# A Mamba-2 and latent attention trunk: the input read in a second, transposed layout, its norms spread by TensorE

## The chip, the cores and the metric

The kernel runs on one core of a Trainium2 chip. The metric is the device time of one execution in microseconds (us), as the median of several runs. A core has TensorE (PE, matrix products, with PEld for its weight loads), VectorE (DVE), ScalarE (ACT), GpSimd (POOL) and SyncE (SP, which here issues most DMAs). Each works through its own queue in order; semaphores tie them together.

## What is computed

A sequence of 2048 tokens of width 1024 passes a Mamba-2 layer and a multi-head latent attention layer, each with an RMS norm ahead and a residual add behind, and a last norm. Only the entry of the Mamba layer matters here:

```python
def rms_norm(x, g):
    y = xf * lax.rsqrt(jnp.mean(xf * xf, axis=-1, keepdims=True) + EPS)
    return (y * g.astype(jnp.float32)).astype(x.dtype)
...
hn = rms_norm(h, g_pre[l])
proj = h @ w_in
z, xBC, dt_raw = jnp.split(proj, [D_INNER, D_INNER + CONV_DIM], axis=-1)
xBC = jax.nn.silu(causal_depthwise_conv(xBC, conv_w, conv_b))
dt = jax.nn.softplus((dt_raw + dt_bias).astype(jnp.float32))
```

The norm of a token is one number, r, by which its whole row is multiplied; g_pre is one number per input channel. Behind the projection come a causal convolution over four tokens, a chunked scan with 32 heads in four groups, a gate SiLU(z), a norm per group and the output projection. Products of float32 accuracy are made of three passes: each factor is split into a high and a low part, and high times high, high times low and low times high are summed (`mm3`, lines 83 to 87).

## The kernel before, in words

The Mamba layer (`mamba`, line 224) takes the tokens in four blocks of 512 (b = 0 to 3), and each block's heads in four groups (g = 0 to 3). The input of a block has to lie with its channels on the partitions, as eight slices k of 128 channels by 512 tokens: `xT`, eight buffers for the high and the low halves.

`load_x` (line 296) loads four row tiles of 128 tokens by 1024 channels (tag `hx`, four buffers), squares them on ScalarE with a sum (line 163), works out r with thirteen small VectorE operations (`rsqrt`, line 139), and multiplies the rows by r on VectorE (line 310). `prep` (line 312) then transposes them: for each slice four TensorE transposes into one PSUM bank (line 171), and from there a split into `xT` by ScalarE (line 111) and VectorE (line 112), which also multiplies by g_pre.

`xbc` (line 324) multiplies the slices with the weight columns of B and C (two channel tiles) and then of x (four channel tiles), each bank of 128 channels by 512 tokens; the weights come through `wraw` (three raw buffers) and are split into `wsp` (six buffers). A finished bank is copied to `craw` (three buffers, line 352), gets the last three tokens of the block before it from `halo` (lines 351 and 353, GpSimd), passes four taps (lines 356 and 358) and SiLU (lines 360 and 361). `zgate` (line 367) does the gate with tokens on the partitions (lines 381 and 382). `steps` (line 416) makes the step sizes of all heads: 16 products with a weight tile `wdt` that is loaded and split once (lines 190, 201, 202, 423), a long chain of small operations, and three products with a triangle and ones (lines 463 to 465). `ssd` (line 479) is the scan, in four chunks of 128 tokens, and begins each chunk with a transpose of B (line 515). `outp` (line 388) multiplies by the output weights and adds into the residual rows `hs`, which are loaded anew from x in the first group of each block (line 394).

The order of the work comes from two places. `mamba` interleaves generators: during the scan of group g of block b it traces the output projection of the group before and the projections of the group after, and in the last but one group of a block also `load_x` (at its start), `prep` and `steps` (at its end) of the next block. The tile framework then plans at build time: it takes that order as the priority, starts what its own estimates of time call ready, and gives the buffers of a tag out in the traced order. On the chip each engine's order is fixed.

## Time and profile before

| | |
|---|---|
| median of 3 runs | 3239.51 us (3238.54 to 3240.34) |
| the profiled execution | 3238.15 us, its span 3236.3 us |
| TensorE busy | 3156.2 us (98%) |
| VectorE busy | 2593.4 us (80%) |
| ScalarE busy | 2055.2 us (64%) |
| GpSimd busy | 646.2 us (20%) |
| granted TensorE clock | 0.995 of full speed |

The span is what the profile sees between the first and the last instruction. A busy time is a union of instruction times, and matmuls overlap, so a busy TensorE need not be at its peak. In the lists of waits, a row says who waited for whom, for how long in total, how often, and the longest. Rows that group instructions give the line, the engine, the operation, the tiles written and read, the count, then the busy time and the mean duration in ns, then the idle time of the engine just before them and who ended it. A line can be that of a helper: every transpose of rows is line 171, every split lines 108 to 112.

### The profile page before, as it was taken

Reading aid. Unit: us, or ns where it says so; the run is one execution under the profiler, and the core shown is the slowest. Engines: PE = TensorE matmul, PEld = TensorE weight load, DVE = VectorE, ACT = ScalarE, POOL = GpSimd, SP = SyncE. Lnnn points to the kernel's source line nnn. Section 1 sums busy time; section 2 is a strip of 40 time slices with the busy share of each in tenths; the row PEclk is TensorE's granted clock in tenths of the full one; section 3 lists DMA queues with packets and bytes.
Section 4 is the critical chain, followed back from the end, with each engine's and each line's share of the span. In section 5 each row is a group of like instructions: output and inputs, shape, how many; then the busy total and the mean of one; then the engine's idle time right before and its main releaser. Section 6 shows DMA issues by size and latency. Waiting matters only on the chain.

```text
span 3236.3 us, 50476 instructions
## 1 busy us (share of the span) xinstructions
PE 3156.2 (98%) x16708; PEld 2563.4 (79%) x16708; DVE 2593.4 (80%) x5490; ACT 2055.2 (64%) x5117; POOL 646.2 (20%) x842
## 2 busy tenths in 40 slices
PE   8999999999999999998999999999999999999998
PEld 6788888888888888887888888777777777777787
DVE  6988888889889888887776765668888888888675
ACT  5666666666657655666555554567777877778522
POOL 1221122221212222222211211222212212223100
PEclk9999999999999999999999999999999999999999
DMA  5333343333433334333466666753443434344385
GB/s 174 108 104 92 118 131 119 105 96 122 140 96 109 90 125 145 104 94 111 132 221 212 236 204 208 246 137 79 82 89 77 97 77 88 77 90 116 81 272 172
DMA packets 210572, 418.91 MB, mean 129 GB/s; under 512 B 27107, under 2 KB 68835, under 8 KB 208869
## 3 DMA queue, kind: packets, MB, share of 16 engines
q1 hardware_dynamic: 168900, 291.39, 28.9%
q0 software_dynamic: 41408, 124.29, 15.7%
q8 instruction: 132, 2.16, 0.3%
q14 instruction: 132, 1.07, 0.1%
HBM read 321.33 MB, written 94.24 MB: 128 GB/s over the span
## 4 chain that ended last, share of the span: by engine, by line
PE 44%; ACT 3%; DMA 2%; DVE 2%; issue 1%; SPq 0%; POOL 0%; ACTq 0%; DVEq 0%
PE mm L85 7%; PE mm L87 7%; PE mm L86 7%; PE tr L933 6%; PE tr L943 3%; PE tr L944 3%; PE tr L86 3%; PE tr L87 3%; PE tr L85 3%; ACT Pr L918 1%; DVE PTs L117 1%; ACT PTs L116 1%; DMA wraw<-in_kv_w_up_dram 1%; PE mm L905 1%; DMA wraw<-in_kv_w_down_dram 0%
## 5 line engine op out<-in xcount | busy, mean ns | idle before, releaser
L117 DVE SCALAR_TENSOR_TENSOR PTs<-tr,PTs 128x512 f16<-128x512 f32 (+3 forms) x640 | 374.7, 607 | 92.6 <-ACT PTs L116 86.0
L116 ACT ACTIVATE PTs<-tr 128x512 f16<-128x512 f32 (+3 forms) x640 | 328.2, 541 | 140.9 <-PE tr L933 140.0
L906 DVE TENSOR_REDUCE mx<-mm 128x1 f32<-128x512 f32 (+2 forms) x631 | 375.5, 607 | 45.4 <-PE mm L87 42.8
L918 ACT ACTIVATE Pr<-mm,nm 128x512 f32<-128x512 f32 (+2 forms) x631 | 395.1, 635 | 23.1 <-DVE nm L910 21.5
L108 ACT ACTIVATE wsp<-wraw 128x512 fp32r<-128x512 f32 (+1 forms) x452 | 251.1, 574 | 171.7 <-PE mm L87 82.4
L109 DVE TENSOR_TENSOR wsp<-wraw,wsp 128x512 fp32r<-128x512 f32 (+1 forms) x452 | 301.8, 680 | 69.7 <-ACT wsp L108 68.9
L85 PE MATMUL mm<-xT,wsp 128*128 128x512 f32 x800 | 321.0, 401 | 0.0
L933 PE MATMUL tr<-pack,Pr 128*128 128x128 f32 x2176 | 317.5, 273 | 0.9 <-ACT Os L950 0.8
L87 PE MATMUL mm<-xT,wsp 128*128 128x512 f32 x800 | 314.1, 393 | 0.0
L86 PE MATMUL mm<-xT,wsp 128*128 128x512 f32 x800 | 312.9, 391 | 0.0
L85 PE MATMUL mm<-K,xT 96*128 96x512 f32 (+2 forms) x639 | 286.7, 449 | 23.1 <-ACT Pr L918 21.7
L933 PEld LDWEIGHTS tr<-pack,Pr 128*128 128x128 f32 x2176 | 253.4, 141 | 49.3 <-ACT Os L950 1.6
L85 PE MATMUL mm<-wsp,xT 128*128 128x512 f32 (+1 forms) x640 | 242.1, 378 | 0.0
L86 PE MATMUL mm<-wsp,xT 128*128 128x512 f32 (+1 forms) x640 | 237.7, 371 | 0.0
L87 PE MATMUL mm<-wsp,xT 128*128 128x512 f32 (+1 forms) x640 | 237.5, 372 | 0.0
L87 PE MATMUL mm<-K,xT 96*128 96x512 f32 (+2 forms) x639 | 231.4, 362 | 0.0
L358 DVE SCALAR_TENSOR_TENSOR cacc<-craw,pack,cacc 128x512 f32<-128x512 f32 x288 | 216.5, 774 | 18.3 <-ACT cacc L356 17.8
L86 PE MATMUL mm<-K,xT 96*128 96x512 f32 (+2 forms) x639 | 231.1, 362 | 0.0
L496 POOL TENSOR_TENSOR Xp<-Xw,Xp 128x512 fp32r<-128x512 f32 x64 | 83.1, 1298 | 697.5 <-ACT Xp L495 393.1
L943 PE MATMUL tr<-PTs,xT 128*128 128x512 f16 (+3 forms) x640 | 222.0, 348 | 0.1
L538 ACT ACTIVATE Xw<-tr,d_wend 128x64 f32<-128x64 f32 x512 | 182.8, 358 | 58.7 <-DVE Xd L534 58.6
L944 PE MATMUL tr<-PTs,xT 128*128 128x512 f16 (+3 forms) x640 | 219.4, 347 | 0.0
(368 smaller groups left out, 8145.9 us busy)
## 6 DMA issues: line engine op xcount, KB each, us to landing
wraw<-in_ssm_w_in_dram SPq DMA_DIRECT2D x256, 256.0 KB, 2.8
big<-cumT SPq DMA_DIRECT2D x64, 512.0 KB, 4.0
wraw<-in_ssm_w_out_dram SPq DMA_DIRECT2D x128, 256.0 KB, 2.6
wraw<-in_ssm_w_in_dram SPq DMA_DIRECT2D x129, 128.0 KB, 2.2
xT<-qn_d POOLq DMA_DIRECT2D x64, 256.0 KB, 4.4
K<-kn_d POOLq DMA_DIRECT2D x15, 1024.0 KB, 9.2
wraw<-in_mla_w_uq_dram SPq DMA_DIRECT2D x36, 256.0 KB, 4.0
hx<-in_x_dram SPq DMA_DIRECT2D x16, 512.0 KB, 4.2
```

Source lines behind the costliest of these rows:

```text
L85: mm(out, l_hi, r_hi, start=start, stop=False)
L86: mm(out, l_hi, r_lo, start=False, stop=False)
L87: mm(out, l_lo, r_hi, start=False, stop=stop)
L108: nc.scalar.activation(hi, src, AF.Copy)
L109: nc.vector.tensor_tensor(lo, src, hi.bitcast(F32), ALU.subtract)
L116: self.nc.scalar.activation(hi, src, AF.Copy, scale=scale)
L117: self.nc.vector.scalar_tensor_tensor(lo, src, scale, hi, ALU.mult, ALU.subtract)
L906: v.tensor_reduce(mx[:, n:n + 1], s[:, :w], AX.X, ALU.max)
L918: nc.scalar.activation(x[:, :w], s[:, :w], AF.Exp, bias=nm, accum_out=sm[:, n:n + 1])
L933: nc.tensor.transpose(pt[:, j * P:(j + 1) * P], st["P"][j][kb], self.ident)
L943: nc.tensor.matmul(st["O"][:, c], vals[h][:, kb, :], u[:, 0], start=kb == 0, stop=False)
L944: nc.tensor.matmul(st["O"][:, c], vals[h][:, kb, :], u[:, 1], start=False, stop=kb == nk - 1)
```

## The change

The host hands the kernel x a second time, transposed (`xT`, 1024 by 2048). `load_xT` takes the place of `load_x` and `prep` in the Mamba layer.

For block 0 the eight transposed slices are loaded straight into pairs of `hx`, multiplied by g_pre in the split, and go into the products without the norm. The rows are loaded behind them, into `hs`, where the residual add uses them too; r comes from them. r is spread over the partitions: four diagonals of r are multiplied by a matrix of ones on TensorE, so that each of the 128 partitions of `rb` holds r of all 512 tokens. The norm is applied after the products: to each conv input on VectorE (24 in the block), to each gate bank on ScalarE through a `craw` buffer (16 in the block), and to the step sizes in place of a copy. The taps of the first B and C are put off until `rb` is there (`later`).

For blocks 1 to 3 the rows are loaded into `hx`, r is worked out and spread into `rb`, then the transposed slices are loaded into the same four buffers, each is multiplied by `rb` on GpSimd, and is split from SBUF. In blocks 2 and 3 the part up to the multiplication is traced a group of heads earlier than the split (`g == G - 3`); in block 1 all of it comes at the end of the last but one group, behind the projections.

The weights of the step sizes are loaded and split once in each block, through `wraw` and `wsp`. The host's code hands over the array; nothing is computed there. The code from the attention on is untouched, and block NB (the input of the second layer) still goes through `load_x` and `prep`.

```diff
     def mamba(self, cp):
-        self.load_x(0, self.a["x"][0:TB])
+        rows, first = self.load_xT(0), self.xbc(0, 0)
+        next(rows)
         self.layer_constants(cp)
-        for part in (self.prep(0, self.g0), self.steps(0), self.xbc(0, 0), self.zgate(0, 0)):
+        for n in range(16):
+            next(rows, None)
+            next(first)
+            if n == 12:
+                while self.later:
+                    self.later.pop(0)()
+        for part in (first, self.steps(0), self.zgate(0, 0)):
...
-            if g == G - 2 and b + 1 < NB:
-                self.load_x(b + 1, self.a["x"][(b + 1) * TB:(b + 2) * TB])
-                parts += [self.prep(b + 1, self.g0), self.steps(b + 1)]
+            if g == G - 3 and 0 < b < NB - 1:
+                ahead = self.load_xT(b + 1)
+                parts.append(islice(ahead, 2))
+                total += 2
+            elif g == G - 2 and b + 1 < NB:
+                parts += [ahead if b else self.load_xT(1), self.steps(b + 1)]
                 total += 3
...
+    def load_xT(self, b):
+        nc, v, t0 = self.nc, self.nc.vector, b * TB
+        rows = [self.a["x"][t0 + i * P:t0 + (i + 1) * P, :] for i in range(4)]
+        def norm(xs):
+            r = self.rows_rms(xs, [self.t(self.sp, "yt", [P, D], BF16, bufs=2) for _ in xs], D)
+            ps = self.t(self.pp, "tr", [P, TB], bufs=4)
+            for i in range(4):
+                d = self.t(self.sp, "CB", [P, P], bufs=2)
+                v.tensor_scalar(d, self.ident, r[:, i:i + 1], None, ALU.mult)
+                nc.tensor.matmul(ps[:, i * P:(i + 1) * P], self.ones, d, start=True, stop=True)
+            rb = self.rb = self.t(self.hh, "rb", [P, TB], bufs=1)
+            nc.scalar.activation(rb, ps, AF.Copy)
+            return r
+        self.xT[b] = []
+        if b:
+            xs = [self.t(self.hh, "hx", [P, D], bufs=4) for _ in range(4)]
+            for x, row in zip(xs, rows):
+                nc.sync.dma_start(x, row)
+            norm(xs)
+            yield
+        raw = []
+        for k in range(KD):
+            if k % 2 == 0:
+                pair = self.t(self.hh, "hx", [P, 2, TB], bufs=4)
+            x = pair[:, k % 2]
+            raw.append(x)
+            last = nc.sync.dma_start(x, self.a["xT"][k * P:(k + 1) * P, t0:t0 + TB])
+            if b:
+                nc.gpsimd.tensor_tensor(x, x, self.rb, ALU.mult)
+            else:
+                if k == 0:
+                    yield
+                self.part(0, k, x)
+                if k:
+                    yield
+        if b:
+            yield
+            for k, x in enumerate(raw):
+                self.part(b, k, x)
+                if k % 4 == 3:
+                    yield
+        if b == 0:
+            self.hs[0] = [self.t(self.hh, "hs", [P, D], bufs=4) for _ in range(4)]
+            for x, row in zip(self.hs[0], rows):
+                with self.tc.issue_after(last.ins):
+                    last = nc.sync.dma_start(x, row)
+                yield
+            v.tensor_copy(self.r0, norm(self.hs[0]))
+            yield
+    def part(self, b, k, x):
+        u = self.t(self.xq, "xT", [P, 2, TB], F32R, bufs=8)
+        self.split(u[:, 0, :], u[:, 1, :], x, self.g0[:, k:k + 1])
+        self.xT[b].append(u)
...
+                def conv():
+                    if b == 0:
+                        nc.vector.tensor_tensor(raw[:, 3:], raw[:, 3:], self.rb, ALU.mult)
...
+                if b + g == 0 and tag == "BC":
+                    self.later.append(conv)
+                else:
+                    conv()
...
+            if b == 0:
+                zn = self.t(self.sp, "craw", [P, TB], bufs=3)
+                nc.scalar.activation(zn, bank, AF.Copy, scale=self.r0[:, i:i + 1])
+                bank = zn
...
     def steps(self, b):
+        raw = self.t(self.wp, "wraw", [P, TB], bufs=WRAW)[:, :KD * H].rearrange("p (k c) -> p k c", k=KD)
+        nc.sync.dma_start(raw, self.a["ssm_w_in"][:, DI + 3072:].rearrange("(k p) c -> p k c", p=P))
+        w = self.t(self.wp, "wsp", [P, 2, TB], F32R, bufs=WSP)[:, 0].rearrange("p (k n h) -> p k n h", k=KD, n=2)
+        self.split(w[:, :, 0], w[:, :, 1], raw)
...
-        nc.scalar.activation(rt, ps[0:2 * H, :], AF.Copy)
+        if b:
+            nc.scalar.activation(rt, ps[0:2 * H, :], AF.Copy)
+        else:
+            v.tensor_tensor(rt, ps[0:2 * H, :], self.rb[0:2 * H], ALU.mult)
```

More of the change, by code (lines that the diff above doesn't have):

```diff
@@ L1 @@
 from contextlib import ExitStack
+from itertools import islice
 import numpy as np
@@ L189, in layer_constants @@
         nc.sync.dma_start(self.pack, a["c_pack"])
-        wdt = self.t(self.wp, "wraw", [P, TB], bufs=WRAW)
-        nc.sync.dma_start(wdt[:, :KD * H].rearrange("p (k c) -> p k c", k=KD),
-                          a["ssm_w_in"][:, DI + 3072:].rearrange("(k p) c -> p k c", p=P))
         self.ones_r = cp.tile([P, P], F32R, name="ones")
@@ L200, in layer_constants @@
         nc.vector.memset(self.mk[:, P:], NEG)
-        self.wdt = cp.tile([P, KD, 2, H], F32R, name="wdt")
-        self.split(self.wdt[:, :, 0], self.wdt[:, :, 1], wdt[:, :KD * H].rearrange("p (k c) -> p k c", k=KD))
         nc.vector.tensor_scalar(self.cw, self.cw, 0.5, None, ALU.mult)
@@ L352, in evacuate @@
                 nc.scalar.activation(raw[:, 3:], bank, AF.Copy)
[L353 to L362 removed]
+                def conv():
+                    if b == 0:
+                        nc.vector.tensor_tensor(raw[:, 3:], raw[:, 3:], self.rb, ALU.mult)
+                    nc.gpsimd.tensor_copy(self.halo[:, ch, :], raw[:, TB:TB + 3])
+                    acc = self.t(self.sp, "cacc", [P, TB], bufs=2)
+                    wk = [self.cw[:, 4 * ch + k:4 * ch + k + 1] for k in range(4)]
+                    nc.scalar.activation(acc, raw[:, 0:TB], AF.Identity, scale=wk[0], bias=self.cb[:, ch:ch + 1])
+                    for k in range(1, 4):
+                        nc.vector.scalar_tensor_tensor(acc, raw[:, k:k + TB], wk[k], acc, ALU.mult, ALU.add)
+                    o = self.t(self.sp, tag, [P, TB], bufs=bufs)
+                    nc.scalar.activation(o, acc, AF.Tanh)
+                    nc.vector.scalar_tensor_tensor(o, o, 1.0, acc, ALU.add, ALU.mult)
+                    outs.append(o)
+                if b + g == 0 and tag == "BC":
+                    self.later.append(conv)
+                else:
+                    conv()
             yield from self.sweep(KD, banks, weights, product, evacuate)
@@ L390, in outp @@
         nc, a, t0 = self.nc, self.a, b * TB
-        if g == 0:
+        if g == 0 and b:
             self.hs[b] = [self.t(self.hh, "hs", [P, D], bufs=4) for _ in range(4)]
@@ L422, in steps @@
             for n in range(2):
-                nc.tensor.matmul(ps[0:2 * H, :], self.wdt[:, k].rearrange("p n h -> p (n h)"), xT[k][:, n, :],
+                nc.tensor.matmul(ps[0:2 * H, :], w[:, k].rearrange("p n h -> p (n h)"), xT[k][:, n, :],
                                  start=k + n == 0, stop=k + n == KD)
```

15 lines of the change are left out of this document (3 added, 12 removed).

## The prediction

> **What bounds the kernel now.** I read the page's busy times first, then what TensorE waited for, then busy times by stretch, and only then the two places that the change touches.
>
> ```profile
> span 3236.3 us, 50476 instructions
> ...
> PE 3156.2 (98%) x16708; PEld 2563.4 (79%) x16708; DVE 2593.4 (80%) x5490; ACT 2055.2 (64%) x5117; POOL 646.2 (20%) x842
> ```
>
> TensorE is busy for 3156.2 of 3236.3 us, so 80.1 us of it are idle. What the change can win is TensorE work taken out, or part of those 80.1 us. The list of TensorE's waits says how much of the idle time lies at the places of the change (columns: total us, times, longest):
>
> ```profile
> PE tr L171 <- DMA wraw<-in_ssm_w_in_dram: 13.6, 1, 13.6
> ...
> PE tr L171 <- DVE st L563: 2.9, 3, 1.3
> ```
>
> Line 171 is the transpose. Before the very first one TensorE stands idle for 13.6 us; before the transposes of the three later token blocks it waits 2.9 us in all. The busy times by stretch (columns: length, then PE, PEld, DVE, ACT, POOL) tell which engine is next in line in the Mamba stage:
>
> ```profile
> 350.00:455.00 105.00, 104.52 (x514) 84.76 (x513) 94.73 (x215) 64.14 (x161) 23.02 (x23) 1.00 0.39 123
> 60.00:350.00 290.00, 286.96 (x1427) 237.75 (x1426) 246.16 (x469) 187.60 (x469) 59.25 (x70) 1.00 0.32 96
> ```
>
> It is VectorE: 246.2 of 290 us (85%) in the first token block, 94.7 of 105 us (90%) across the boundary to the second. TensorE loses 3.0 us in the one and 0.5 us in the other. VectorE at 90% therefore does not yet hold TensorE up, and that figure is the yardstick for the work that the change adds to VectorE.
>
> **The start (block 0).** In order of time, from the timeline of the first 60 us (start, duration, engine, line):
>
> ```profile
> 0.74 1.81 SPq L301 DMA_DIRECT2D hx<-in_x_dram  x4
> ...
> 9.85 0.21 DVE L203 TENSOR_SCALAR pack<-pack 128x96 f32<-128x96 f32 x1 [8.62 <-DMA pack<-in_c_pack_dram]
> ...
> 13.61 3.51 PE L171 MATMUL tr<-pack,hx 128*128 128x128 f32 x16 [13.61 <-DMA wraw<-in_ssm_w_in_dram]
> ...
> 19.92 3.87 PE L423 MATMUL tr<-xT,wdt 128*64 128x512 f32 x16
> ...
> 33.08 0.58 ACT L352 ACTIVATE craw<-mm 128x512 f32<-128x512 f32 x1
> ```
>
> Today the rows of x come in, are squared, scaled and transposed, and only then multiplied; the first finished bank of B and C leaves at 33.08. Afterwards the first product needs only the constants (g0 lies in them), the first 256 KB of the transposed x and one weight slice. Their landing times are bounded by these rows (the first 20 us by stretch, last column GB/s, before it the busy share; then issue to landing of three kinds of DMA in the first 40 us):
>
> ```profile
> 0.00:20.00 20.00, 6.39 (x38) 5.89 (x39) 10.30 (x42) 13.97 (x28) 0.64 (x7) 1.00 0.79 266
> ...
> hx<-in_x_dram SPq DMA_DIRECT2D x8, 512.0 KB, 4.2
> ...
> pack<-in_c_pack_dram SPq DMA_DIRECT2D x1, 323.0 KB, 7.2
> ```
>
> 266 GB/s at a busy share of 0.79 is an estimated 337 GB/s while the queues are full. The 0.7 MB ahead of the first product (256 KB of x, 323 KB of constants, 128 KB of weights) takes 2.1 us at that rate; issued at 0.74 with the latency of the 512 KB row, 4.2, it has landed by 4.9; if the constants again take 7.2 from an issue near 1.2, at 8.4. One split on ScalarE and VectorE follows (0.61 + 0.80 by rows further below). First product: 6 us, at most 9.8. I take 6, because the constants now stand second in the queue and not behind 2 MB. That is 7.6 us earlier (at worst 3.8).
>
> From 13.61 to 33.08 TensorE also does work that goes or stays. It stays for 45 products (two channels, eight slices, three passes, less the last three of the second bank) and the 16 of line 423, which take 3.87, so 0.24 each: 61 x 0.24 = 14.6 us. The other 4.9 us are 32 transposes and the gaps between their evacuations, and they go. What comes in their place: four products of a 128x128 matrix of ones with a diagonal.
>
> ```profile
> 369.01 0.38 PE L463 MATMUL tr<-big,pack 128*128 128x128 f32 x2
> 369.23 0.39 PE L464 MATMUL tr<-big,ones 128*128 128x128 f32 x2
> ...
> 369.68 0.27 PE L515 MATMUL tr<-pack,BC 128*128 128x128 f32 x1
> ```
>
> Line 464 is just such a product; it is two instructions and holds TensorE for 0.22 us (369.01 to 369.23), so four cost 0.9. They wait for the squares and the chain of small VectorE operations, but the products of the x channels stand ready beside them. One wait is added: the rows of x for the norms (2 MB, issued right behind the transposed x) run ahead of the later B and C weights, which have only three raw buffers. 2 MB at 337 GB/s is 6 us; bounds 0 to 6, and I take 3, since up to three slices are loaded before. Start: -7.6 - 4.9 + 0.9 + 3 = **-8.7 us**.
>
> **The three boundaries (blocks 1 to 3).** The price of a transpose is not its duration but the distance to the next:
>
> ```profile
> 734.98 1.47 PE L171 MATMUL tr<-pack,hx 128*128 128x128 f32 x12
> ```
>
> Twelve in 1.47 us, the last 0.27 long like line 515 above: 1.2/11 = 0.109 us each, 32 of them 3.5 us. With 2.9 us of waits over three boundaries and 0.9 us of new products at each, TensorE gets 3 x 3.5 + 2.9 - 3 x 0.9 = 10.7 us back, about 3.6 each. The Trainium skill's page "TensorE: Matmul & The Clock Gate", section "Part 4: PE-mode transpose", puts a transpose in a kernel at about 275 ns; the trace agrees for the duration (0.27), not for what a row of them costs. By that figure the 128 transposes of all blocks would be worth 21 us more than by 0.109; twelve in 1.47 us speak so plainly against it that it gets no chance of its own.
>
> For blocks 2 and 3 the rest is covered: the norms and the multiplied rows are done a group of heads early, and the splits read SBUF when the last gate products free the xT buffers. Two boundaries: **-7.2 us**.
>
> Block 1 is different. Its loads are issued early (the rows need nothing), but its norm now stands behind the last group's z products instead of a group before, because block 0 still uses its own spread norm until there. From the squares to the norm's first use the trace shows:
>
> ```profile
> 242.41 1.04 ACT L163 ACTIVATE yt<-hx 128x1024 bf16<-128x1024 f32 x1
> ...
> 253.64 2.74 DVE L310 TENSOR_SCALAR hx<-hx,rsy 128x1024 f32<-128x1024 f32 x4
> ```
>
> That is 11.2 us. Then diagonals, products and the copy (some 3 us), then eight multiplications on GpSimd, one after the other:
>
> ```profile
> L496 POOL TENSOR_TENSOR Xp<-Xw,Xp 128x512 fp32r<-128x512 f32 x12 | 15.7, 1308 | 119.9 <-ACT Xp L495 67.4 <-issue 26.2 <-PE mm L87 21.6
> ```
>
> 8 x 1.31 = 10.5 us, then the last split, 1.4: 26 us in a line. TensorE has the output products of the group before it (96 x 0.24 = 23 us), and the first xT slice is there after 17 us, so the B and C products do not starve. But the step sizes of block 1 (line 423 and the chain to line 465) come late, and the scan of the last heads queues behind their PSUM banks: its first transpose, line 515 at 369.68, follows line 465 at once. If the squares begin near 340 the chain ends near 385, 15 us later than 369.7. VectorE must then do the scan in less time; over that stretch it has 105 - 94.7 = 10.3 us free. The rest, 4.7 us, I charge to TensorE (bounds 0 and 15). Block 1: -3.6 + 4.7 = **+1.1 us**.
>
> **Block 0's norms after the products.** 24 conv inputs are multiplied on VectorE, 16 gate banks copied with a scale on ScalarE. The nearest rows, of 60 to 345 us:
>
> ```profile
> L358 DVE SCALAR_TENSOR_TENSOR cacc<-craw,pack,cacc 128x512 f32<-128x512 f32 x63 | 48.4, 795 | 2.5 <-ACT cacc L356 2.4
> ...
> L567 DVE TENSOR_TENSOR y<-y,sz 128x512 f32<-128x512 f32 x12 | 10.3, 858 | 0.2
> ```
>
> ```profile
> L352 ACT ACTIVATE craw<-mm 128x512 f32<-128x512 f32 x19 | 11.3, 608 | 1.7 <-PE mm L87 1.7
> ```
>
> 24 x 0.86 = 20.6 us more on VectorE, 16 x 0.61 = 9.7 us on ScalarE. VectorE goes from 246.2 to 266.8 of 290 us, 92%: two points over the stretch that cost TensorE nothing. Bounds 0 and 20.6; I take **+2.5 us**, near the lower end, as that stretch is the nearest row.
>
> **Costed at nothing.** The 24 GpSimd multiplications, 31 us, lie in three blocks where GpSimd is busy for 23 of 105 us; without that cover the halves for the scan come late (a rival below). The step weights, now loaded and split once per block, are 128 KB, an issue of 0.45 us on SP (1.81/4) and a small split. The transposed loads add eight issues per block, 3.6 us on SP, and each pair waits for a squared row's buffer; the weight loads queued behind them on SP are covered by three raw and six split buffers, each four-channel slice of which feeds TensorE for 12 x 0.24 = 2.9 us. On VectorE twelve scalings of 0.69 (2.74/4) go; twelve small diagonals come.
>
> **Sum.** -8.7 - 7.2 + 1.1 + 2.5 = -12.3 us. The profiled execution took 3238.15, 1.4 below the median 3239.51: 3225.9 by the profile, **3227** beside the median.
>
> **Rivals.** That the transposes stay is excluded by the code.
> - The start is bound by the DMA: the constants land at 8.4 and the rows cost the full 6 us. 3.8 + 3 more: 3234. For it: the busy share of 0.79 in the first 20 us. Against: the constants move up in the queue.
> - Block 1's chain holds the scan by its full 15 us: 10.3 more, 3237. For it: line 515 right behind line 465. Against: VectorE has other work to bring forward.
> - Slower: the three conv buffers (craw) of block 0. Each is now held for the multiplication too, and the gate copies use the same three. The fourth bank of a four-channel sweep waits until the first channel's multiplication and three taps are through, 0.86 + 3 x 0.795 = 3.2 us, and TensorE needs the banks for the next sweep. Two sweeps in each of four groups: 8 x 3.2 = 26 us instead of 2.5, so 3250. It passes 3246 from 2.7 us per sweep. For it: VectorE's 92%. Against: banks are asked for one after another, 3 x 6 x 0.24 = 4.3 us between the first and the fourth.
> - Slower too: GpSimd's multiplications stop VectorE for their whole 1.31 us and TensorE pays it all, 24 x 1.31 = 31 us, 3258; it passes 3246 from 0.8 us each. Line 567, which has two SBUF inputs, takes 0.86 on average here, so some stopping shows; but VectorE has 10 us free even at a boundary. The Trainium skill's page "SBUF — State Buffer", section "Who interferes with whom", speaks for this: a VectorE operation with two SBUF inputs and a GpSimd one that reads SBUF lock each other out for a whole instruction.
> - Faster still: nothing is charged for block 1 and block 0, and the rows cost no wait at the start: -4.7 - 2.5 - 3, 3217.
>
> **How the numbers follow.** A measurement of this kernel can tell about 0.2%, 6.5 us: faster means below 3233, slower above 3246. The forecast (3218 to 3233) 0.58, the faster case 0.07, the start 0.10, block 1's scan 0.12, the conv buffers 0.10, GpSimd's lock 0.03. Faster 0.65, same 0.22, slower 0.13. The range 3212 to 3243 reaches past both middle rivals and leaves out the slower ones and a little below.
>
> **What would show it.** Right: the first product near 6 us, the first B and C evacuation near 21, line 381's fourth evacuation of block 0 about 9 us earlier; no PE gap over 2 us at the later two boundaries; the scan of the last heads in block 0 starting near 385. Wrong: TensorE waits on ScalarE's conv or gate copies through block 0, VectorE times well over 0.86 beside GpSimd's multiplications, or new waits in the stages after Mamba, which I hold unchanged.

## The result, and the profile after

The changed kernel is slower: 3263.22 us (median of 4 runs, 3261.16 to 3268.82) against 3239.03 in the same comparison, ratio 1.0078 (95% interval 1.0061 to 1.0096). The profiled execution took 3262.28 us. The page's first lines after the change, with the counterparts of those shown of before:

```profile
span 3260.4 us, 50376 instructions
...
PE 3159.5 (97%) x16612; PEld 2555.9 (78%) x16612; DVE 2610.0 (80%) x5511; ACT 2065.4 (63%) x5135; POOL 682.3 (21%) x866
```

TensorE has 96 instructions fewer and yet 3.3 us more busy time, and its idle time went from 80.1 to 100.9 us. VectorE's total rose by 16.6 us, GpSimd's by 36.1. The list of what TensorE waited for up to the end of the Mamba layer (0 to 1345 us; total us, times, longest):

```profile
PE mm L86 <- ACT xT L112: 7.4, 1, 7.4
PE tr L506 <- DVE xT L113: 5.0, 8, 0.8
PE mm L88 <- DVE wsp L110: 4.9, 2, 4.7
PE tr L316 <- DVE CB L315: 4.8, 2, 2.7
PE tr L658 <- DVE y L653: 4.7, 2, 3.3
```

The 13.6 us at the start are 7.4 now, as meant. But behind it stand rows whose releaser is VectorE every time. Three are new: the splits of the new input (L113), a weight split (L110) and the diagonals of the norm (L315). The fourth, the gated rows of the scan (L653), was worth 1.0 us before.

To see where the loss arises I compared the start times of instructions that both kernels have: the tanh of a group's last gate bank (z), and the first transpose of B that begins a group's scan (scan). Differences to before in us; (b,g) is block and group. The last three columns are kernels of the experiments: F is e17, M is e19, K is e20. Each column is one profiled execution, and K's was the shortest of its eleven.

| moment | before | after | F | M | K |
|---|---|---|---|---|---|
| last x bank of (0,0) copied | 59.8 | -10.8 | -11.9 | -11.3 | -11.7 |
| z (0,0) | 80.1 | -3.5 | -2.5 | -3.4 | -4.8 |
| z (0,3) | 343.8 | +3.5 | +3.1 | +3.0 | -1.9 |
| scan (1,0) | 451.9 | +15.8 | +16.1 | +4.7 | -0.7 |
| z (1,2) | 642.2 | +15.7 | +16.2 | +4.8 | -0.5 |
| z (1,3) | 735.8 | +22.8 | +23.6 | +6.6 | +2.5 |
| scan (2,0) | 844.3 | +19.3 | +19.4 | +2.5 | -1.6 |
| z (2,2) | 1034.6 | +18.4 | +19.4 | +2.7 | -1.4 |
| z (2,3) | 1128.5 | +25.5 | +26.9 | +5.1 | +1.1 |
| scan (3,0) | 1239.1 | +19.5 | +21.1 | 0.0 | -4.9 |
| span | 3236.3 | +24.1 | +24.9 | +2.9 | -3.0 |

Read down the column "after": 10.8 us are won at the start, 7.3 of them are given back before the first group is through, another 7.0 in the rest of block 0, 12.3 at the boundary to block 1, and some 7 in the second group's stage of blocks 1 and 2, where the norms of blocks 2 and 3 now lie. Only the boundaries to blocks 2 and 3 give something back, 3.5 and 6.0. The 7.0 of block 0 hang on the planned order too: in the ten experiments whose block 0 is written the same they are 4.0 to 6.6.

**The boundary to block 1.** Busy times by stretch, before and then changed (length, PE, PEld, DVE, ACT, POOL, granted clock, DMA share, GB/s):

```profile
345.00:445.00 100.00, 99.00 (x498) 80.34 (x497) 91.62 (x202) 63.69 (x159) 23.02 (x23) 1.00 0.39 123
```

```profile
345.00:445.00 100.00, 87.31 (x413) 67.66 (x412) 87.47 (x196) 60.99 (x145) 29.01 (x30) 0.97 0.40 127
```

TensorE was busy for 99.0 of these 100 us before and is for 87.3 now. What happened is in the changed kernel's timeline; first GpSimd, then the last two of VectorE's eight splits (start, us, engine, line):

```profile
356.12 12.67 POOL L336 TENSOR_TENSOR hx<-hx,rb 128x512 f32<-128x512 f32 x8 [3.73 <-DMA wraw<-in_ssm_w_out_dram]
```

```profile
367.89 1.45 DVE L113 SCALAR_TENSOR_TENSOR xT<-hx,pack,xT 128x512 fp32r<-128x512 f32 x1 [0.24 <-ACT xT L112]
369.58 0.75 DVE L113 SCALAR_TENSOR_TENSOR xT<-hx,pack,xT 128x512 fp32r<-128x512 f32 x1 [0.24 <-ACT xT L112]
```

Eight multiplications run on GpSimd until 368.79. Six of the splits beside them take VectorE 1.45 us each; the last one, which begins behind them, takes 0.75. Between 358.2 and 370.3 VectorE does eight splits and nothing else. TensorE's row L506 <- DVE xT L113 is the same thing seen from its side: the step products come at steps of 1.69 us. Up to 417.50 TensorE then waits 4.7 us for one weight split of VectorE, which is busy without a gap there, and the clock falls. That this wait is a late effect of the slow splits is argued, not shown; it is gone in e4, which has no multiplications but also another planned order. Busy times and the granted clock (third number from the end) around the waits that end at 135 and 417 us, changed kernel:

```profile
134.00:141.00 7.00, 5.89 (x20) 5.04 (x21) 5.14 (x10) 4.60 (x9) 0.00 (x0) 0.51 0.36 112
414.00:421.00 7.00, 3.50 (x9) 2.78 (x10) 7.00 (x20) 5.08 (x19) 0.18 (x1) 0.51 0.28 78
```

The clock is at 0.51 for these 7 us, where before it was 1.00 in both stretches. The Trainium skill's page "TensorE: Matmul & The Clock Gate", section "Part 1: The HAM clock gate (the "warmup" mystery)", says that an idle window of some 3.4 us halves the clock; the trace agrees, with waits of 3.3 and 4.7 us. Waits of 2.1 and 2.7 us in the same kernel (second group's stage of blocks 1 and 2) left it at 1.00. So a wait of the long kind costs more than its length.

**VectorE in the second group's stage.** There the eight multiplications run from 666.60 to 678.71. VectorE's timeline beside them:

```profile
671.46 1.72 DVE L113 SCALAR_TENSOR_TENSOR wsp<-wraw,pack,wsp 128x512 fp32r<-128x512 f32 x1
673.10 0.74 DVE L488 SCALAR_TENSOR_TENSOR hs<-mm,rr,hs 128x512 f32<-128x512 f32 x1
...
676.05 0.68 DVE L637 TENSOR_TENSOR yt<-tr,d_ecum 128x512 f32<-128x512 f32 x1
...
677.48 1.78 DVE L638 TENSOR_TENSOR y<-y,yt 128x512 f32<-128x512 f32 x1
```

The first and the last read two tiles in SBUF; without a GpSimd operation beside them they take 0.75 and 0.68 us (medians of the same trace). The two between read one tile from PSUM (`mm`, `tr`) and are as fast as ever. Against such medians VectorE's operations beside the 24 multiplications took 4.4, 3.2 and 3.2 us longer in the three blocks, an estimate of 10.9 us in all.

### The profile page after: what moved, and what is told of

Same layout as the page of the kernel before. It is cut to its first block, busy times and chain, and to the rows that moved or that the text cites. A ratio compares the mean times of both kernels' runs of the same rounds, so it can differ in the third digit from the quotient of the medians.

```text
span 3260.4 us, 50376 instructions
## 1 busy us (share of the span) xinstructions
PE 3159.5 (97%) x16612; PEld 2555.9 (78%) x16612; DVE 2610.0 (80%) x5511; ACT 2065.4 (63%) x5135; POOL 682.3 (21%) x866
## 4 chain that ended last, share of the span: by engine, by line
PE 43%; ACT 3%; DMA 3%; DVE 2%; issue 1%; SPq 0%; POOL 0%; ACTq 0%; DVEq 0%; POOLq 0%
PE mm L86 7%; PE mm L88 7%; PE mm L87 7%; PE tr L1019 6%; PE tr L1029 3%; PE tr L1030 3%; PE tr L87 3%; PE tr L88 3%; PE tr L86 3%; ACT Pr L1004 1%; DVE PTs L118 1%; DMA os<-ri_d 1%; DMA wraw<-in_mla_w_in_dram 1%; ACT PTs L117 1%; PE mm L991 1%
## 5 line engine op out<-in xcount | busy, mean ns | idle before, releaser
L110 DVE TENSOR_TENSOR wsp<-wraw,wsp 128x512 fp32r<-128x512 f32 (+1 forms) x456 | 303.1, 676 | 76.3 <-ACT wsp L109 74.9
```

The costliest lines, as they stand in the source:

```text
L110: nc.vector.tensor_tensor(lo, src, hi.bitcast(F32), ALU.subtract)
```

## The experiments

Eighteen kernels ran. Each ratio is against the kernel before in the same comparison, whose median went from 3239.0 to 3242.3 us over the six comparisons; a difference between the times of two experiments can be off by up to 3 us for that alone. The framework plans every kernel anew, so an edit can also move work that it does not name. The letters in the expectations: T, the loss is the sum of places read from the table above; U, block 0's VectorE work and conv buffers are nearly all of it; V, GpSimd's multiplications stop VectorE; W, the moved step products and gate copies; X, the transposed loads delay weights; Y, the place of the norm in the traced order; the rest are told where they arise.

**Which blocks cost.** In e1 blocks 1 to 3 take the old path, so only block 0 is new:

```diff
-            if g == G - 3 and 0 < b < NB - 1:
-                ahead = self.load_xT(b + 1)
-                parts.append(islice(ahead, 2))
-                total += 2
-            elif g == G - 2 and b + 1 < NB:
-                parts += [ahead if b else self.load_xT(1), self.steps(b + 1)]
+            if g == G - 2 and b + 1 < NB:
+                self.load_x(b + 1, self.a["x"][(b + 1) * TB:(b + 2) * TB])
+                parts += [self.prep(b + 1, self.g0), self.steps(b + 1)]
```

> Block 0 as in the changed kernel; blocks 1 to 3 are scaled, transposed and split as before the change (load_x, prep). Theory T (the loss is the sum of three places: +13 us at the boundary to block 1, where the step products are issued slice by slice behind GpSimd; +14 us in block 0 behind a start that is 10.8 us early; +6 us twice where the norms of blocks 2 and 3 are spread, -3 us twice at their boundaries): the block 0 part alone gives before + 3, 3242 +- 5. Theory U (VectorE's and the craw buffers' extra load in block 0 is nearly all of it): 3255 or more. Theory V (the 24 GpSimd multiplications stop VectorE, about 31 us): 3230.

Measured: 3243.6 us, 1.0011 (1.0002 to 1.0020), as T has it. Block 0 is not nearly all of it; U falls, and so does V with its 3230.

In e2 it is block 0 that takes the old path; its norms behind the products go with it:

```diff
-        rows, first = self.load_xT(0), self.xbc(0, 0)
...
-        for part in (first, self.steps(0), self.zgate(0, 0)):
+        for part in (self.prep(0, self.g0), self.steps(0), self.xbc(0, 0), self.zgate(0, 0)):
```

> Block 0 is loaded, normed, transposed and split as before the change and nothing is multiplied after its products; blocks 1 to 3 as in the changed kernel. T: 13 + 2 x 3 above before, 3258 +- 5, with no gain at the start. U: 3239 or below. V: 3262 or more.

Measured: 3253.65 us, 1.0040 (1.0025 to 1.0055). Blocks 1 to 3 alone lose 13 us, at the lower edge of T's range; U and V fall. With e1's 3 that is 16 of 24 us, so the parts do not simply add.

e3 does block 1's norm, loads and multiplications with the second group of heads, as in the later blocks, with two spread norms in bfloat16 (two of its edits):

```diff
-            if g == G - 3 and 0 < b < NB - 1:
+            if g == G - 3 and b < NB - 1:
...
-            rb = self.rb = self.t(self.hh, "rb", [P, TB], bufs=1)
+            rb = self.rb = self.t(self.hh, "rb", [P, TB], BF16, bufs=2)
```

> The changed kernel with two buffers for the spread norm (kept in 16 bits so that they fit: the norms are rounded), and block 1's norm, loads and multiplications issued with the second group of heads like those of blocks 2 and 3. T: the 13 us at the boundary to block 1 become the 3 that blocks 2 and 3 pay: 3253 +- 4. U and V: 3263, since block 0's VectorE work and the GpSimd multiplications are all there.

Measured: 3258.89 us, 1.0048 (1.0031 to 1.0064), 2 us past T's range. The boundary now wins 4.2 us (15.6 at z (0,3), 11.4 at scan (1,0)), but from z (0,0) to z (0,3) block 0 loses 20.0 instead of 7.0: the moved work is not free where it goes.

e4 leaves GpSimd's multiplications out:

```diff
-                nc.gpsimd.tensor_tensor(x, x, self.rb, ALU.mult)
+                pass
```

> The changed kernel without the 24 GpSimd multiplications: blocks 1 to 3 go into the products without their norm (the norms are still worked out and spread). T: the seven waits of the step products in block 1 go and its chain is some 10 us shorter: 3251 +- 5. V: 31 us less, 3232. U: 3263.

Measured: 3253.47 us, 1.0038 (1.0025 to 1.0052). 10 us less, as T has it; V's 3232 falls. Nearly all of it comes from block 1's boundary, where the loss falls from 12.3 to 2.7 us, although TensorE now waits 5.2 us for the diagonals of the norm there. The second group's stage goes on losing, 6.3 and 9.1 us (7.1 each in the changed kernel). The splits of that boundary now take 746 ns instead of 1305 (changed kernel first, then e4; 345 to 445 us):

```profile
L113 DVE SCALAR_TENSOR_TENSOR xT<-hx,pack,xT 128x512 fp32r<-128x512 f32 x8 | 10.4, 1305 | 2.4 <-ACT xT L112 2.4
```

```profile
L113 DVE SCALAR_TENSOR_TENSOR xT<-hx,pack,xT 128x512 fp32r<-128x512 f32 x8 | 5.9, 746 | 0.0
```

**Block 0's multiplications.** e5 is e1 without the 24 multiplications of the conv inputs; e7 is e1 with them on GpSimd:

```diff
-                        nc.vector.tensor_tensor(raw[:, 3:], raw[:, 3:], self.rb, ALU.mult)
+                        nc.gpsimd.tensor_tensor(raw[:, 3:], raw[:, 3:], self.rb, ALU.mult)
```

> Base is e1 (block 0 as changed, blocks 1 to 3 as before). Block 0's 24 multiplications of conv inputs on VectorE are left out, so its B, C and x channels lack the norm. T, now for block 0 alone (the multiplications stand in front of the scan's operations on VectorE, TensorE waits for those and then runs at half clock for a window): e1 less 6 to 8, 3236. Rival W (the gate copies through craw, or the step products that moved behind the first products, cost it): 3243, as e1.

Measured: 3236.57 us, 0.9984 (0.9975 to 0.9993), 7 us below e1. The multiplications are the cost in block 0; W falls.

> Base is e1. The 24 multiplications of block 0 run on GpSimd instead of VectorE. T: GpSimd is at 20 per cent there, VectorE is relieved: 3237 +- 3. V for block 0 (a GpSimd multiplication stops VectorE for as long): 3243 or more. W: 3243.

Measured: 3261.16 us, 1.0052 (1.0036 to 1.0069), 18 us above e1 (16 if each is taken against its own kernel before). T missed by 24 us; V for block 0, 3243 or more, is what is left. The groups of e1 and then e7 in 60 to 350 us:

```profile
L425 DVE SCALAR_TENSOR_TENSOR cacc<-craw,pack,cacc 128x512 f32<-128x512 f32 x54 | 41.2, 792 | 0.3 <-ACT cacc L423 0.3
...
L419 DVE TENSOR_TENSOR craw<-craw,rb 128x512 f32<-128x512 f32 x18 | 12.0, 679 | 1.0 <-ACT craw L416 1.0
```

```profile
L425 DVE SCALAR_TENSOR_TENSOR cacc<-craw,pack,cacc 128x512 f32<-128x512 f32 x56 | 49.3, 906 | 3.7 <-ACT cacc L423 3.7
...
L419 POOL TENSOR_TENSOR craw<-craw,rb 128x512 f32<-128x512 f32 x18 | 23.9, 1330 | 23.3 <-ACT craw L416 23.2
```

One multiplication is 679 ns on VectorE and 1330 on GpSimd, which in e1 was busy for 59.7 of these 290 us; still it is dearer there. It lengthens each conv chain, and the taps grow from 792 to 906 ns. How the 18 us divide between the two was not tested.

**The second group's stage.** Why the norms of blocks 2 and 3 cost 7 us each took several kernels. e8 leaves out their spreading (diagonals, products with ones, copy):

```diff
         def norm(xs):
             r = self.rows_rms(xs, [self.t(self.sp, "yt", [P, D], BF16, bufs=2) for _ in xs], D)
+            if b > 1:
+                return r
```

> The changed kernel without the diagonals, the products of ones and the copy for blocks 2 and 3: these blocks are multiplied by block 1's spread norm. T for the 6 us at the second group of heads (TensorE stands in those products until VectorE has worked out the norm, and the scan's banks stand behind them): 2 x 5 to 6 less, 3252 +- 3. Rival X (the 2 MB of transposed loads, queued on SP ahead of the output weights, cost it): 3263.

Measured: 3265.13 us, 1.0071 (1.0056 to 1.0086).

e9 issues their transposed loads and multiplications at the start of the next group's stage:

```diff
-                parts.append(islice(ahead, 2))
-                total += 2
+                parts.append(islice(ahead, 1))
+                total += 1
             elif g == G - 2 and b + 1 < NB:
+                if b:
+                    parts.insert(0, islice(ahead, 1))
+                    total += 1
```

> The changed kernel with the norms of blocks 2 and 3 where they are, but their transposed loads and multiplications traced at the start of the next group's work. X: the weights are no longer behind the loads, 2 x 4 to 6 less, 3253 +- 3. T: 3263 +- 2, the products of ones still wait.

Measured: 3261.41 us, 1.0061 (1.0046 to 1.0076).

e10 issues norm, loads and multiplications of blocks 2 and 3 behind the last pieces of the scan:

```diff
-                parts.append(islice(ahead, 2))
-                total += 2
...
             for _ in scan:
                 pass
+            if g == G - 3 and 0 < b < NB - 1:
+                for _ in islice(ahead, 2):
+                    pass
```

> The changed kernel, only that the norms, loads and GpSimd multiplications of blocks 2 and 3 are issued behind the last pieces of the scan of the second group of heads instead of ahead of them: the same instructions in another order. Theory Y (the place in the order: the norm's four squares and their scratch tiles stand ahead of the scan's last piece, which the output projection and the next scan wait for; that is the 6 us that the changed kernel loses in the second group of heads of blocks 1 and 2): 2 x 5.5 us go, 3252 us, and the rows around the first scan step of (1,2) and (2,2) come out as in the kernel before. Theory G (the GpSimd multiplications beside VectorE are what costs there, wherever they stand): 3261 to 3263 us, no gain.

Measured: 3261.39 us, 1.0065 (1.0052 to 1.0079).

e12 is e10, and the splits and step products of each boundary come behind the scan too:

```diff
-                parts += [ahead if b else self.load_xT(1), self.steps(b + 1)]
-                total += 3
...
+            if g == G - 2 and b + 1 < NB:
+                for part in (ahead if b else self.load_xT(1), self.steps(b + 1)):
+                    for _ in part:
+                        pass
```

> As the kernel above, and at each of the three block boundaries the splits of the transposed input and the step products are issued behind the last pieces of the scan too. Theory Y: the same order effect holds at the boundaries, some 2 us each, so 5 us below the kernel above, 3247 us. Rival (the splits were late, not early: at block 1 the step products wait slice by slice for splits that GpSimd's multiplications pace): standing later they hold TensorE longer, 2 to 4 us at each boundary, 3258 to 3264 us.

Measured: 3258.97 us, 1.0058 (1.0042 to 1.0073).

None moved the time by more than its interval leaves room for. T's reason for that stage (by e8), X (by e9) and Y fell; e10 came out as G has it, by which the GpSimd multiplications cost there wherever they stand, and e12 as its rival has it. All four kernels keep those multiplications. The waits show that something is always in the way: e10 and e9 keep the wait for the diagonals (2.1 and 2.7 us in the changed kernel), and e8, which has none, waits for VectorE elsewhere. TensorE's waits near the second group's stage, in e10, e9 (640 us on) and e8 (1030 us on):

```profile
PE tr L317 <- DVE CB L316: 2.9, 2, 1.8
```

```profile
PE tr L634 <- issue: 3.2, 1, 3.2
PE tr L319 <- DVE CB L318: 1.5, 1, 1.5
```

```profile
PE mm L86 <- DVE sz L463: 5.6, 1, 5.6
PE tr L633 <- DVE Xd L622: 0.8, 1, 0.8
```

**A block 0 without its second cost.** e13 folds the gate norm of e1 into the scale of the tanh and into the later product with the scan's rows; e14 also lets VectorE multiply straight out of PSUM.

```diff
-            if b == 0:
-                zn = self.t(self.sp, "craw", [P, TB], bufs=3)
-                nc.scalar.activation(zn, bank, AF.Copy, scale=self.r0[:, i:i + 1])
-                bank = zn
-            nc.scalar.activation(sz, bank, AF.Tanh, scale=0.5)
+            nc.scalar.activation(sz, bank, AF.Tanh, scale=0.5 if b else self.rh[:, i:i + 1])
```

> Block 0 alone in the new way (blocks 1 to 3 as in the kernel before: 3243.6 us, 1.0011, when it ran), with its gate norm folded in: the row factor goes into the scale of the tanh and into the later product of the gate with the scan's rows, so the 16 ScalarE copies into the buffers that the convolution uses are gone and no work is left out. Theory T (VectorE's 24 multiplications are the cost in block 0, ScalarE and the buffers are not): 0 to 2 us less, 3242 us, ratio 1.0005. Theory C (the copies take the convolution's three buffers, which paces the products): 4 to 5 us less, 3239 us, ratio 0.9995.

Measured: 3240.88 us, 1.0001 (0.9992 to 1.0009), between T's 3242 and C's 3239.

```diff
-                nc.scalar.activation(raw[:, 3:], bank, AF.Copy)
+                late = b + g == 0 and tag == "BC"
+                if b or late:
+                    nc.scalar.activation(raw[:, 3:], bank, AF.Copy)
+                else:
+                    nc.vector.tensor_tensor(raw[:, 3:], bank, self.rb, ALU.mult)
```

> As the kernel above, and VectorE multiplies straight out of the product's bank into the convolution's buffer (but for the first two banks, whose factor isn't there yet), so that 22 ScalarE copies are gone too and VectorE has as many multiplications as before. Theory T: what VectorE does is unchanged, the chain from the bank to the taps is a copy shorter: 1 us less than the kernel above, 3241 us, ratio 1.000. Rival (VectorE runs in bursts and now holds the banks that TensorE needs): TensorE waits for banks, 6 to 10 us more, 3249 us.

Measured: 3241.07 us, 1.0001 (0.9992 to 1.0010). Both lie at the kernel before. The intervals of e1 and e13 overlap, so whether the conv buffers play a part stays open; e14 shows no cost of banks held by VectorE and no gain.

**What is left.** e15 gives block 1 its old path:

```diff
-                parts += [ahead if b else self.load_xT(1), self.steps(b + 1)]
+                if b == 0:
+                    self.load_x(1, self.a["x"][TB:2 * TB])
+                parts += [ahead if b else self.prep(1, self.g0), self.steps(b + 1)]
```

> The changed kernel, only that block 1 is read, scaled and transposed as in the kernel before; blocks 0, 2 and 3 stay new. No work is left out. Theory S (the places add up: +13 us at block 1's boundary, which now costs what it did before, and the rest stays): 3263 - 13 = 3250 us. Rival R (the loss is spread over GpSimd, VectorE and throttle stretches and only shows at that boundary): 3258 to 3262 us.

Measured: 3249.65 us, 1.0023 (1.0014 to 1.0032). S holds: that boundary is worth 13 to 14 us.

e16 keeps GpSimd's work but takes it off the chain:

```diff
-                nc.gpsimd.tensor_tensor(x, x, self.rb, ALU.mult)
+                off = self.t(self.hh, "off", [P, TB // 2], BF16, bufs=1)
+                for s in (slice(0, TB // 2), slice(TB // 2, TB)):
+                    nc.gpsimd.tensor_tensor(off, x[:, s], self.rb[:, s], ALU.mult)
```

> The changed kernel, only that GpSimd writes its 24 products (as 48 of half the size) into a scratch tile and the splits read the raw rows, so the norms of blocks 1 to 3 are left out of the result; GpSimd's work and its place in time stay, but nothing waits for it. Without the multiplications at all the kernel took 3253.5 us. Theory P (what they cost is the wait in the chain, norm, multiplication, split, step product): 3253 us here too. Theory L (what they cost is that VectorE is slowed beside them): 3261 to 3264 us, as the changed kernel.

Measured: 3262.84 us, 1.0063 (1.0047 to 1.0078). P falls, and the time is the one that L expected: nothing waits for the products any more, and the time is the same. (At block 1's boundary the loss is 9.0 us instead of 12.3, so a part there was the chain; the half-size form was also somewhat longer in sum, 42.1 us for 48 against 36.9 for 24.)

e17 (column F) issues, in blocks 2 and 3, the norm's chain behind the scan of the second group, and diagonals, products with ones, loads and multiplications behind the next output products:

```diff
-                parts.append(islice(ahead, 2))
-                total += 2
             elif g == G - 2 and b + 1 < NB:
+                if b:
+                    parts.insert(1, islice(ahead, 2))
+                    total += 2
...
+            if g == G - 3 and 0 < b < NB - 1:
+                next(ahead)
...
-            norm(xs)
+            if b == 1:
+                norm(xs)
+            else:
+                v.tensor_copy(self.r0, self.rows_rms(xs, [self.t(self.sp, "yt", [P, D], BF16, bufs=2) for _ in xs], D))
+                yield
+                spread(self.r0)
```

> The changed kernel, only that in blocks 2 and 3 the norm (squares and the small chain) is issued behind the scan of the second group of heads, and the diagonals, the products with ones and the multiplied loads behind the next output products, so that TensorE does not come to the products before their diagonals are there. Theory Q (TensorE's order: it stands 2 to 3 us before the products with ones for the small chain, and with the norm in front of the scan's last piece it waits for that instead; both have to go): some 5 us less in each of two blocks, 3253 us. Theory R (the work itself, wherever it stands): 3261 us.

Measured: 3263.49 us, 1.0072 (1.0055 to 1.0088). Q falls. TensorE no longer waits before the products with ones, but the loss is there, a little later, with a new releaser. Its waits in 640 to 720 us, and GpSimd's timeline:

```profile
PE tr L87 <- POOL Xp L590: 3.1, 1, 3.1
PE tr L639 <- DVE Xd L628: 0.8, 1, 0.8
```

```profile
685.88 11.82 POOL L344 TENSOR_TENSOR hx<-hx,rb 128x512 f32<-128x512 f32 x8 [4.73 <-ACT rb L321]
697.66 1.71 POOL L590 TENSOR_TENSOR Xp<-Xw,Xp 128x512 fp32r<-128x512 f32 x1
```

GpSimd's own part of the scan (the low half of Xp, L590) stands in its queue behind eight multiplications of 11.8 us together, and TensorE waits for it.

e18 joins the parts: e13's edit of block 0, e15's of block 1 and e17's of blocks 2 and 3.

> The parts that the traces show as gains or as free: block 0 new with its gate norm folded (by itself 3240.9 us), block 1 as before, blocks 2 and 3 new with the products later as in the kernel above. No work is left out. Theory Q: two boundaries at 3.6 us less than before and little lost in the second group: 3235 us, ratio 0.998. Theory R: the second group costs as much as the boundaries give, and more: 3243 to 3245 us, ratio 1.001.

Measured: 3251.45 us, 1.0028 (1.0018 to 1.0038), as R has it or worse. So in the second group's stage two things may each suffice: products that TensorE meets too early, and GpSimd's multiplications. e17 had removed the first, e4 the second, never both. e19 (column M) is e17 with the edit of e4, so without the multiplications; e20 (column K) is e18 with those of blocks 2 and 3 on VectorE:

```diff
-                nc.gpsimd.tensor_tensor(x, x, self.rb, ALU.mult)
+                v.tensor_tensor(x, x, self.rb, ALU.mult)
```

> As the kernel with the products later (3263.5 us), and GpSimd's 24 multiplications are left out, so the norms of blocks 1 to 3 are left out of the result. Theory M (in the second group of heads two things each suffice for the loss: TensorE in front of the products with ones, and GpSimd's multiplications in front of GpSimd's own step of the scan, for which TensorE waits 3.1 us; with both away it goes): 10 us less at block 1's boundary, as without the multiplications, and some 5 us less in each of two blocks, 3243 us. Theory R (the second group loses as much without them): 3253 us.

Measured: 3241.08 us, 1.0001 (0.9992 to 1.0010). M holds: 22.4 us less than e17 (21 if each is taken against its own kernel before), and nothing but the 24 multiplications is gone from the work. The second group's stage loses 1.8 and 2.4 us now, 7.4 and 7.5 in e17.

> As the version made of the kept parts (3251.5 us: block 0 new with its gate norm folded, block 1 as before, blocks 2 and 3 new with the products later), only that the 16 multiplications of blocks 2 and 3 are done by VectorE instead of GpSimd. No work is left out. Theory M: GpSimd's scan step is no longer held up, VectorE has some 3 us more per block than with its four row scalings before: 3237 us, ratio 0.9985. Rival (VectorE is as full as GpSimd is slow: eight multiplications in a row hold up its part of the scan): 3250 us.

Measured: 3239.31 us, 0.9998 (0.9989 to 1.0008). M's 3237 is missed by 2 us, its rival's 3250 by 11: 12 us less than e18 with the same work done. What TensorE waits for in 600 to 780 us is down from 5.2 us in e18 to 2.3, and a multiplication takes VectorE less than half of GpSimd's time:

```profile
PE tr L558 <- DVE big L556: 1.1, 1, 1.1
PE tr L322 <- DVE CB L321: 0.7, 1, 0.7
PE tr L515 <- DVE xT L113: 0.5, 1, 0.5
```

```profile
L347 DVE TENSOR_TENSOR hx<-hx,rb 128x512 f32<-128x512 f32 x8 | 4.9, 686 | 0.2 <-ACT rb L324 0.2
```

e20 is the best version that leaves no work out, and it cannot be told from the kernel before.

## Why the prediction was wrong

The forecast was 3227 us with a range of 3212 to 3243; the kernel took 3263. The step that failed is the first sentence under "Costed at nothing": "The 24 GpSimd multiplications, 31 us, lie in three blocks where GpSimd is busy for 23 of 105 us". They are worth 22.4 us when the order leaves no other wait in front of them (e17 to e19), and 10 in the order of the change itself (e4). The cover was judged by GpSimd's own idle time. What mattered was VectorE beside them and GpSimd's queue behind them. The sentence goes on to name the second, that the scan's halves come late without that cover, but the rival to which it points prices only the first. The rival "GpSimd's multiplications stop VectorE" said 3258, the nearest figure in the text, and had a chance of 0.03. Its mechanism is seen; its size is less than it assumed, 0.7 us for most of block 1's splits (1.45 beside, 0.75 behind) and an estimate of 10.9 us over the 24 instead of 31. That its 3258 lies near 3263 is luck in part, since the start and the norms of block 0 missed too. The trace agrees in direction with the rule of the Trainium skill cited there ("SBUF — State Buffer", "Who interferes with whom"): a split that read PSUM took 742 ns on average over all blocks before, and one that reads SBUF beside GpSimd takes 1.45 us. The change moved the splits' source from PSUM to SBUF, the prediction says so, and did not follow it up.

By place, the 36 us between the forecast and the measurement are roughly 5 at the start, 5 in block 0, 11 at block 1's boundary, 12 in and at blocks 2 and 3, and 4 behind the layer. The prediction's other steps:

- **Start, -8.7** (its terms add up to -8.6). The first product came at 7.41 (6 said, 9.8 at most), the first B and C evacuation at 21.16 (21 said), and the last x bank 10.8 us early. The 21 is in part luck: the sum kept the 16 step products (3.87 us) ahead of that evacuation, and the change moves them behind the last x products. The first product, 1.4 us later than said, and the 45 products ahead of the evacuation, 13.5 us instead of 10.8, made up for it. The step products were still to come: they, two waits of 0.7 and 1.4 us in the chain behind them, and the copy of the last gate bank ahead of its tanh (0.67) are 6.6 of the 7.3 us given back. At the end of the first group's gate -3.5 are left. The transposes did go as said; the term is 5 us too large.
- **Boundaries of blocks 2 and 3, -7.2.** At the boundaries themselves 3.5 and 6.0 us are won, 9.5 in all and more than said, and no wait of TensorE there exceeds 1.7 us ("no PE gap over 2 us"). "The rest is covered" was wrong: the norms a group of heads earlier cost 7 us each.
- **Block 1, +1.1.** 12.3. The place and the kind of wait were right (the scan of the last heads began at 387.7 instead of 369.7, near 385 was said), but with the 3.6 us that were to be won there the cost is 15.9, just past the bounds of 0 to 15. The 4.7 chosen rested on VectorE's 10.3 us of free time, of which the slow splits took 4.4, and left out that a long wait of TensorE halves its clock (0.51 around 417 us).
- **Block 0's norms, +2.5.** 7.0 from z (0,0) to z (0,3); without the multiplications none (e5: -0.8 and -0.9). One took 0.68 us, not 0.86. VectorE was busy for 247.8 of 290 us, hardly more than before and less than the 266.8 forecast: the average over the stretch did not show the bursts. VectorE's timeline of the changed kernel ahead of the 3.3 us for which TensorE waits at 135.11 shows one, two multiplications and six taps in front of the scan's gated rows:

```profile
127.48 1.28 DVE L422 TENSOR_TENSOR craw<-craw,rb 128x512 f32<-128x512 f32 x2
...
129.28 5.09 DVE L428 SCALAR_TENSOR_TENSOR cacc<-craw,pack,cacc 128x512 f32<-128x512 f32 x6
134.29 0.68 DVE L653 TENSOR_TENSOR y<-y,sz 128x512 f32<-128x512 f32 x1
```

- **Conv buffers.** The slow rival with 0.10 was not it: TensorE has no wait on ScalarE's conv or gate copies in 60 to 350 us, and e13, which takes the gate copies out of those buffers, is 3 us below e1, with intervals that overlap.
- **Behind Mamba.** The layer ends 20 us late and the span is 24 us longer. In the other kernels, whose code there is the same, that remainder is between -1.0 and 8.9 us; its cause stays open.

How the 22.4 us divide between VectorE slowed and GpSimd's queue is not settled. e16 shows that the chain through the splits is not needed for the loss, and e17 shows one wait of 3.1 us on the queue. In e17 VectorE's operations beside the multiplications took an estimate of 11.6 us longer, found as above; how much of that TensorE pays is not known, and no kernel separates the two everywhere.

## What to carry over

An engine that is 20% busy is not free. Before work is given to it, list what its queue holds behind that work and who waits for it, and which operations of other engines take longer beside it; then price the moved work by the busiest of them, not by the idle one. When taking one wait away moves the time by nothing, take two away together before dropping the cause.

## What the runs showed of the hardware

- A VectorE split of 128x512 with two SBUF sources took 0.75 us by itself and 1.45 beside a GpSimd multiplication, an addition of two SBUF tiles 0.68 and 1.78; VectorE operations with one source in PSUM took 0.68 and 0.74 us beside it, no longer than elsewhere.
- GpSimd's multiplication in turn averaged 1571 ns over the 24 (1308 for the nearest operation before), while VectorE does the same multiplication in 686.
- After TensorE waits of 3.3 and 4.7 us in an otherwise full stretch, the granted clock stood at 0.51 over 7 us; after waits of 2.1 and 2.7 us it stayed at 1.00.
- At the very start the products came at half rate too, the first two at distances of 0.79 and 0.59 us and those behind them at 0.43, against 0.23 later, though the rows of the profile give a granted clock of 1.00 there.
